# Key parts of a head pair by one copy, one subtraction and six transfers; value low parts in one operation; probability rows 4 to 11 scaled by GpSimd instead of ScalarE

## The chip, the cores and the metric

One NeuronCore of a Trainium2 chip. The metric is the device time of one execution in microseconds (us): the median of 3 runs before the change is 721.15 us (719.63 to 722.5). The engines have short names: PE is TensorE, DVE VectorE, ACT ScalarE, POOL GpSimd, SP SyncE (it only issues transfers here). Each engine has its own stream of instructions and works through it in order; semaphores hold an instruction back until what it reads is there.

## The reference

One transformer block on 512 tokens of width 1024, all in float32. Layer norm, a modulation computed from a condition vector, one input projection; then eight heads of dilated attention (group A) and eight heads of three-branch attention (group B: compressed, selected and window keys); output projection, residual, layer norm; a gated feed-forward layer of width 2816 with a causal convolution; residual and layer norm.

```python
mod = silu(c) @ w_ada + b_ada
u = layer_norm(x) * (1 + sc1) + sh1
qa, ka, va, qb, kc, vc, ksl, vsl, kw, vw, gl = split(u @ w_in)
o_a = dilated_attention(rope(qa), rope(ka), va)
o_b = nsa_attention(rope(qb), rope(kc), vc, rope(ksl), vsl, rope(kw), vw, gl, ...)
x = layer_norm(ALPHA * x + g1 * (concat(o_a, o_b) @ w_o), ln1_g, ln1_b)
u = layer_norm(x) * (1 + sc2) + sh2
a_gate, a_val = split(u @ w_up)
h = gelu(causal_dwconv(a_gate)) * a_val
x = layer_norm(ALPHA * x + g2 * (h @ w_down), ln2_g, ln2_b)
```

## The kernel before, in words

**Split products.** A float32 product is made of three matmuls (`mm3`): each operand is split into a high part (a copy rounded to the narrower type fp32r) and a low part (the operand less its high part), and high times high, high times low and low times high are added up in PSUM. The high part is made by ACT with a copy, the low part by DVE or POOL with a subtraction that reads the high part.

**Stages.** Up to about 52 us the first projection (tile `first`). From there to about 313 us the attention: the rest of the input projection (`quad`, in chunks of 48 matmuls of 256 columns), the rows of attention, and at the end the first output tile. Then output projection, feed-forward (`pg`, `pvv`) and down projection (`d`).

**Rows.** A row is one head, one kind of keys and one or two tiles of 128 queries: 12 rows for each head pair of group B, 6 for each of group A. A row goes through steps: `scores` (PE, lines 707 and 708: queries against `khh` and `kll`), `weights` (DVE, line 715: mask, minimum along the row), `power` (ACT, line 721), `scale` (DVE reciprocal at line 726, then the product with one over the sum and the gate: on ACT at line 732 with one more DVE operation at line 730 where `r['act']` is set, otherwise in one POOL operation at line 736), `turn` (PE transposes, line 741), `parts` and `rest` (ACT and DVE, lines 760 and 764: high and low part of the turned row) and `use` (PE, line 789: products with the values). `SEQ` at line 154 says in which order one round of the loop at line 1303 runs the steps of different rows; `scale` runs one round and `turn` three rounds behind `weights`. Score tiles have two PSUM banks (tag `s`), so the scores of a row start when a bank has been read.

**Key tiles.** A pair of heads shares one PSUM tile `pt`, head 0 on partitions 0 to 63, head 1 on 64 to 127. The scores need for each head a tile `khh` with the head's high part on both halves of the partitions, and a tile `kll` with its low part on both. `k_half` (line 474) makes them for one head: ACT copies 64 partitions (line 478), DVE subtracts on the same 64 (line 480), and one transfer each, issued on SP, brings the half to the other 64 partitions. `k_stack` (line 490) does it for both heads: the two pairs of group B at lines 1284 and 1287; `a_post` (line 945) for the four pairs of group A, one head in each step.

**Value tiles.** `v_split` (line 501) makes, for two heads, high, low, low, high blocks of 64 columns: one ACT copy and two DVE subtractions (lines 505 and 506), twelve times in all (`vb`, `va`).

**Order.** The program is emitted by loops with fillers between the steps (`fill_one`, `run_misc`), and the framework's scheduler sets the final order on every engine. SP's queue carries the weight loads and the key transfers in one stream. The loads of `ada_col` feed reductions on DVE (line 1033), which stand in DVE's stream between the rows' operations.

Of the kernel before, what the change touches and what calls it, by code (L numbers as in the profile page):

```python
# [14 lines left out]
AF = mybir.ActivationFunctionType  # L15
# [91 lines left out]
def body(ctx, tc, nc, a, out, dbg=None):  # L107
# [59 lines left out]
    V, A, P, T = nc.vector, nc.scalar, nc.gpsimd, nc.tensor  # L167
# [58 lines left out]
    def acc_done():  # L226
        live[0] -= 1
# [8 lines left out]
    def f(x):  # L236
        return x.bitcast(F32)

    def load(dst, src, queue=nc.sync):
        queue.dma_start(dst, src)  # L240
# [114 lines left out]
    _, uh, ul = u_parts()  # L355
# [110 lines left out]
    def q_stack(pt, mk=t2):  # L466
# [4 lines left out]
        V.tensor_sub(o[0:64], pt[64:128], f(o[64:128]))  # L471
        return e, o

    def k_half(pt, e, mk=t2, spare=True):
        b, c0 = 64 * e, 64 - 64 * e
        if spare:
            hh, ll = mk('khh'), mk('kll')
            A.activation(hh[b:b + 64], pt[b:b + 64], AF.Copy)
            load(f(hh[c0:c0 + 64]), f(hh[b:b + 64]))
            V.tensor_sub(ll[b:b + 64], pt[b:b + 64], f(hh[b:b + 64]))  # L480
            load(f(ll[c0:c0 + 64]), f(ll[b:b + 64]))
            return hh, ll
        hh, ll = mk('khh'), mk('kll')
        A.activation(hh[b:b + 64], pt[b:b + 64], AF.Copy)
        A.activation(hh[c0:c0 + 64], pt[b:b + 64], AF.Copy)
        V.tensor_sub(ll[b:b + 64], pt[b:b + 64], f(hh[b:b + 64]))
        V.tensor_copy(ll[c0:c0 + 64], f(ll[b:b + 64]))
        return hh, ll

    def k_stack(pt, mk=t2):  # L490
        return [k_half(pt, e, mk) for e in range(2)]


    gates = cst.tile([128, NT, 24], F32, name='gates')
# [6 lines left out]
    def v_split(dst, src, n):  # L501
        s4 = src.rearrange("p (n e d) -> p n e d", e=2, d=64)
        d4 = dst.rearrange("p (n s d) -> p n s d", s=4, d=64)
        A.activation(d4[:, :, 0:4:3, :], s4, AF.Copy)
        V.tensor_sub(d4[:, :, 1, :], s4[:, :, 0, :], f(d4[:, :, 0, :]))
        V.tensor_sub(d4[:, :, 2, :], s4[:, :, 1, :], f(d4[:, :, 3, :]))


    def blocks_of(src, eng, res):
# [435 lines left out]
    def a_post(j):  # L945
        mk = to if j == 0 else t2

        def run(banks):
# [15 lines left out]
            pt = transposed(ys, 1, 'acc')  # L964
            wlive[0] -= 2
            yield 2
            ka[j] = []
            for b in range(2):
                ka[j].append(k_half(pt, b, mk))
                if b == 1:  # L970
                    acc_done()
                    ready.add(('a', j))
                yield
        return run

    def a_head(j, e):
# [317 lines left out]
        start_misc(late_steps(GAP, st_))  # L1294
    nrow = len(rows)
    for k, r in enumerate(rows):
        r['act'] = 4 <= k < 20
    rows[0]['scores']()
    wo_started = [False]
    wo_fill = wo_first()  # L1300
# [261 lines left out]
```

## Time and profile before

| | us |
|---|---|
| median of 3 runs | 721.15 (719.63 to 722.5) |
| the profiled execution | 724.09 |
| its span, first to last instruction | 722.3 |
| PE busy in the span | 692.0 |
| DVE, ACT, POOL busy | 459.2, 347.3, 238.7 |

The profiled execution is one more execution of the same program; its span leaves out 1.8 us around the first and the last instruction. A timeline row gives start, duration, engine, line and operation; a bracket at its end gives how long the engine had been idle before it and what ended that. A row of a table of stretches gives busy time and count of instructions for each engine in a stretch, then the granted share of TensorE's full clock, the busy share of the 16 DMA engines and what they moved.

### The profile page before, as it was taken

What the parts mean: (1) busy time and instruction counts of PE and PEld (TensorE: products, weight loads), DVE (VectorE), ACT (ScalarE), POOL (GpSimd) and SP (SyncE); (2) the same over time, 40 slices, a digit from 0 to 9 for tenths busy, and PEclk for the clock granted to TensorE, in tenths of its full rate; (3) what the DMA queues carried; (4) which work ended last, traced back from release to release, by engine and by line L of the source; (5) the groups of instructions that cost most, each with busy time, mean ns of one, the idle gap of its engine ahead of it and who ended that gap; (6) DMA issues with size and microseconds to landing.
All of it is one profiled execution on the core that took longest, in us unless ns stands there. A gap on an engine that the chain in (4) does not pass through costs nothing.

```text
span 722.3 us, 10901 instructions
## 1 busy us (share of the span) xinstructions
PE 692.0 (96%) x3964; PEld 598.6 (83%) x3964; DVE 459.2 (64%) x965; ACT 347.3 (48%) x706; POOL 238.7 (33%) x252
## 2 busy tenths in 40 slices
PE   8999899899989998999999999999999999999995
PEld 7999689897889886778898888888888788888884
DVE  7879877767886989978844444554543363445236
ACT  5657487744567588916553333333433341232101
POOL 2002510342466484512310110111110355765326
PEclk8999999999999999999999999999999999999999
DMA  9967741256451212350112233444423233434002
GB/s 343 386 207 197 208 144 68 59 204 234 146 204 60 59 61 87 130 192 1 59 59 88 88 100 133 142 147 148 146 91 114 88 110 123 139 123 136 10 15 102
DMA packets 31069, 93.07 MB, mean 129 GB/s; under 512 B 4132, under 2 KB 4900, under 8 KB 31016
## 3 DMA queue, kind: packets, MB, share of 16 engines
q1 hardware_dynamic: 30580, 92.20, 37.8%
q8 instruction: 31, 0.51, 0.3%
q10 hardware_dynamic: 436, 0.18, 0.1%
q14 instruction: 22, 0.18, 0.1%
HBM read 87.13 MB, written 2.10 MB: 124 GB/s over the span
## 4 chain that ended last, share of the span: by engine, by line
PE 75%; DVE 11%; ACT 5%; POOL 3%; issue 3%; DMA 2%; POOLq 0%; SPq 0%; DVEq 0%; ACTq 0%
PE d L261 6%; PE d L260 6%; PE d L259 6%; PE pvv L259 5%; PE pvv L261 5%; PE pvv L260 5%; PE pg L259 5%; PE pg L261 5%; PE pg L260 5%; PE first L393 3%; PE quad L259 3%; PE quad L260 2%; PE quad L261 2%; PE pT L741 2%; PE hid L1160 2%
## 5 line engine op out<-in xcount | busy, mean ns | idle before, releaser
L256 DVE TENSOR_TENSOR wlo<-wraw,whi 128x1024 fp32r<-128x1024 f32 x60 | 83.7, 1395 | 122.6 <-ACT whi L255 121.4
L255 ACT ACTIVATE whi<-wraw 128x1024 fp32r<-128x1024 f32 x60 | 63.6, 1060 | 139.9 <-PE pg L260 68.1
L259 PE MATMUL quad<-whi,u 128*128 128x256 f32 x256 | 75.8, 296 | 1.0 <-DVE qo L471 1.0
L260 PE MATMUL quad<-wlo,u 128*128 128x256 f32 x256 | 73.1, 286 | 0.0
L261 PE MATMUL quad<-whi,u 128*128 128x256 f32 x256 | 73.0, 285 | 0.0
L1514 POOL TENSOR_TENSOR wraw<-wraw,arow 128x1024 f32<-128x1024 f32 x22 | 58.9, 2688 | 37.0 <-DMA wraw<-w_down 35.8
L259 PE MATMUL pg<-u,whi 128*128 128x512 f32 (+1 forms) x176 | 67.7, 385 | 0.0
L260 PE MATMUL pg<-u,whi 128*128 128x512 f32 (+1 forms) x176 | 66.8, 380 | 0.0
L261 PE MATMUL pg<-u,wlo 128*128 128x512 f32 (+1 forms) x176 | 66.8, 379 | 0.0
L261 PE MATMUL pvv<-u,wlo 128*128 128x512 f32 (+1 forms) x176 | 66.8, 379 | 0.0
L259 PE MATMUL pvv<-u,whi 128*128 128x512 f32 (+1 forms) x176 | 66.8, 379 | 0.0
L260 PE MATMUL pvv<-u,whi 128*128 128x512 f32 (+1 forms) x176 | 66.8, 379 | 0.0
L256 POOL TENSOR_TENSOR hl<-cv,hh 128x512 fp32r<-128x512 f32 x14 | 23.8, 1704 | 110.6 <-ACT hh L255 110.6
L259 PEld LDWEIGHTS quad<-whi,u 128*128 128x128 f32 x256 | 49.5, 193 | 5.8 <-issue 3.9
L260 PEld LDWEIGHTS quad<-wlo,u 128*128 128x128 f32 x256 | 49.5, 193 | 1.1 <-issue 0.4
L715 DVE CUSTOM_DVE_ANT_0 p<-sp,masks 128x128 f32<-128x128 f32 (+1 forms) x96 | 44.6, 482 | 8.6 <-PE sp L708 8.2
L261 PEld LDWEIGHTS quad<-whi,u 128*128 128x128 f32 x256 | 49.5, 193 | 0.1
L741 PE MATMUL pT<-ident,p 128*128 128x128 f32 x240 | 39.9, 280 | 7.4 <-POOL p L736 4.1
L260 PEld LDWEIGHTS pg<-u,whi 128*128 128x128 f32 x176 | 33.1, 188 | 6.7 <-issue 0.5
L259 PEld LDWEIGHTS pg<-u,whi 128*128 128x128 f32 x176 | 33.1, 188 | 6.5 <-issue 0.5
L261 PEld LDWEIGHTS pg<-u,wlo 128*128 128x128 f32 x176 | 33.1, 188 | 6.3
L260 PEld LDWEIGHTS pvv<-u,whi 128*128 128x128 f32 x176 | 33.1, 188 | 6.2
(650 smaller groups left out, 1855.3 us busy)
## 6 DMA issues: line engine op xcount, KB each, us to landing
wraw<-w_up SPq DMA_DIRECT2D x44, 512.0 KB, 3.2
wraw<-w_down SPq DMA_DIRECT2D x22, 512.0 KB, 3.3
ada<-ada_col SPq DMA_DIRECT2D x32, 256.0 KB, 5.8
wraw<-w_quad SPq DMA_DIRECT2D x16, 512.0 KB, 4.3
wraw<-ada_col SPq DMA_DIRECT2D x16, 512.0 KB, 4.3
wraw<-ada_row SPq DMA_DIRECT2D x16, 512.0 KB, 3.3
x<-x SPq DMA_DIRECT2D x8, 512.0 KB, 4.9
wraw<-w_o SPq DMA_DIRECT2D x8, 512.0 KB, 3.2
```

The costliest lines, as they stand in the source:

```text
L255: A.activation(hi, raw, AF.Copy)
L256: lo_engine.tensor_sub(lo, raw, f(hi))
L259: T.matmul(o_, sh, mh, start=start, stop=False)
L260: T.matmul(o_, sh, ml, start=False, stop=False)
L261: T.matmul(o_, sl, mh, start=False, stop=stop)
L393: T.matmul(o_, l[:, tk], r[:, cs], start=(j == 0 and t % 2 == 0 and x == 0 and term is terms[0]), stop=(j == KD - 1 and t % 2 == 1 and x = ...
L715: V.tensor_tensor_reduce(p[:, cols[i]], e['s'][:, cols[i]], masks[:, m0:mask0 + 512], 1.0, 3e38, op0=ALU.add, op1=ALU.min, accum_out=m_[:, ...
L741: T.transpose(e['t'][:, 128 * j:128 * j + 128], e['p'][:, 128 * j:128 * j + 128], ident)
L1160: T.matmul(acc[0:62, 0:256], bl[l_ // 8][:, l_ % 8, :], w[:, l, :], start=l_ == 0, stop=l_ == 15)
L1514: P.tensor_mul(w, w, g2)
```

## The change

Three edits. (1) `k_pair` makes the tiles of both heads of a pair together: ACT copies all 128 partitions of `pt` into the second head's high tile, DVE subtracts all 128 into the second head's low tile, and six transfers spread them: for high and low each, the lower half goes to both halves of the first head's tile, and then the upper half of the second head's tile goes over its own lower half. That third transfer overwrites what the first two read, so it waits until both have landed. `a_post` now calls it in one step, frees the PSUM bank there, and says that the pair is ready one step later. (2) `v_split` subtracts both low blocks in one DVE operation. (3) `r['act']` is set for rows 12 to 19 instead of 4 to 19, so rows 4 to 11 are scaled at POOL's line.

```diff
--- before.py
+++ after.py
@@ -471,6 +471,17 @@
         V.tensor_sub(o[0:64], pt[64:128], f(o[64:128]))
         return e, o
 
+    def k_pair(pt, mk=t2):
+
+        a_, b_ = [mk('khh') for _ in range(2)], [mk('kll') for _ in range(2)]
+        A.activation(a_[1], pt, AF.Copy)
+        V.tensor_sub(b_[1], pt, f(a_[1]))
+        for x in (a_, b_):
+            for h in range(2):
+                load(f(x[0][64 * h:64 * h + 64]), f(x[1][0:64]))
+            load(f(x[1][0:64]), f(x[1][64:128]))
+        return list(zip(a_, b_))
+
     def k_half(pt, e, mk=t2, spare=True):
         b, c0 = 64 * e, 64 - 64 * e
         if spare:
@@ -488,7 +499,7 @@
         return hh, ll
 
     def k_stack(pt, mk=t2):
-        return [k_half(pt, e, mk) for e in range(2)]
+        return k_pair(pt, mk)
 
 
     gates = cst.tile([128, NT, 24], F32, name='gates')
@@ -502,8 +513,7 @@
         s4 = src.rearrange("p (n e d) -> p n e d", e=2, d=64)
         d4 = dst.rearrange("p (n s d) -> p n s d", s=4, d=64)
         A.activation(d4[:, :, 0:4:3, :], s4, AF.Copy)
-        V.tensor_sub(d4[:, :, 1, :], s4[:, :, 0, :], f(d4[:, :, 0, :]))
-        V.tensor_sub(d4[:, :, 2, :], s4[:, :, 1, :], f(d4[:, :, 3, :]))
+        V.tensor_sub(d4[:, :, 1:3, :], s4, f(d4[:, :, 0:4:3, :]))
 
 
     def blocks_of(src, eng, res):
@@ -964,13 +974,11 @@
             pt = transposed(ys, 1, 'acc')
             wlive[0] -= 2
             yield 2
-            ka[j] = []
-            for b in range(2):
-                ka[j].append(k_half(pt, b, mk))
-                if b == 1:
-                    acc_done()
-                    ready.add(('a', j))
-                yield
+            ka[j] = k_pair(pt, mk)
+            acc_done()
+            yield
+            ready.add(('a', j))
+            yield
         return run
 
     def a_head(j, e):
@@ -1294,7 +1302,7 @@
         start_misc(late_steps(GAP, st_))
     nrow = len(rows)
     for k, r in enumerate(rows):
-        r['act'] = 4 <= k < 20
+        r['act'] = 12 <= k < 20
     rows[0]['scores']()
     wo_started = [False]
     wo_fill = wo_first()
```

The scheduler's order moves with it. Lines from 482 on have other numbers in the changed program (before/after): 1033/1041, 1125/1133, 715/725, 736/746, 519/529; 480 becomes 478.

SP's queue around the two pairs of group B, before:

```order
L240 DMA wraw<-ada_col 128x1024
L240 DMA khh<-khh 64x512
L240 DMA kll<-kll 64x512
L240 DMA khh<-khh 64x512
L240 DMA kll<-kll 64x512
L240 DMA khh<-khh 64x512
L240 DMA wraw<-w_quad 128x1024
L240 DMA kll<-kll 64x512
L240 DMA khh<-khh 64x512
L240 DMA kll<-kll 64x512
L240 DMA wraw<-ada_col 128x1024 x2
```

and now:

```order
L240 DMA wraw<-ada_col 128x1024
L240 DMA khh<-khh 64x512 x2
L240 DMA kll<-kll 64x512 x2
L240 DMA wraw<-w_quad 128x1024
L240 DMA khh<-khh 64x512
L240 DMA kll<-kll 64x512
L240 DMA khh<-khh 64x512 x2
L240 DMA kll<-kll 64x512 x2
L240 DMA wraw<-ada_col 128x1024
L240 DMA khh<-khh 64x512
L240 DMA kll<-kll 64x512
L240 DMA wraw<-ada_col 128x1024
```

The first two transfers of high and low parts now stand together, and the third ones behind a load of weights (`w_quad`, `ada_col`).

DVE in the same place, before (`kll` is the subtraction for keys, `qe` and `qo` for queries, the operation that writes `wraw,mod` a reduction over `ada_col`, `p,sa__982` the first row's weights):

```order
L1033 ISA wraw,mod<-wraw,crow,b_col 128x1024
L1033 ISA mod 128x1
L480 TENSOR_TENSOR kll<-qT,khh 64x512
L1125 TENSOR_TENSOR wlo<-wraw,whi 128x512
L470 TENSOR_TENSOR qe<-qT,qe 64x512
L471 TENSOR_TENSOR qo<-qT,qo 64x512
L480 TENSOR_TENSOR kll<-qT,khh 64x512
L1033 ISA wraw,mod<-wraw,crow,b_col 128x1024
L1033 ISA mod 128x1
L480 TENSOR_TENSOR kll<-qT,khh 64x512
L470 TENSOR_TENSOR qe<-qT,qe 64x512
L471 TENSOR_TENSOR qo<-qT,qo 64x512
```

and now:

```order
L1041 ISA wraw,mod<-wraw,crow,b_col 128x1024
L1041 ISA mod 128x1
L1133 TENSOR_TENSOR wlo<-wraw,whi 128x512
L1041 ISA wraw,mod<-wraw,crow,b_col 128x1024
L1041 ISA mod 128x1
L470 TENSOR_TENSOR qe<-qT,qe 64x512
L471 TENSOR_TENSOR qo<-qT,qo 64x512
L478 TENSOR_TENSOR kll<-qT,khh 128x512
L1133 TENSOR_TENSOR wlo<-wraw,whi 128x512
L725 ISA p,sa__982<-sp,masks 128x128
L725 ISA sa__982 128x1
L725 ISA p,sa__982<-sp,masks 128x256
```

Of three key subtractions in this piece one is left (a fourth stands just ahead of it in both orders, as 64 and now as 128 partitions). The second reduction stands before the queries' subtractions instead of behind them, a subtraction of weights (`wlo`) has come in behind the keys, and the second pair of `qe` and `qo` has gone behind the weights of the first two rows.

POOL around 200 us (`p` of the first rows of the third head pair; `wlo` is the low part of a weight chunk), before:

```order
L736 TENSOR_SCALAR p<-p,sa__2447 128x128
L736 TENSOR_SCALAR p<-p,sa__2447 128x256
L736 TENSOR_SCALAR p<-p,sa__2478 128x384
L1125 TENSOR_TENSOR wlo<-wraw,whi 128x512 x2
L736 TENSOR_SCALAR p<-p,sa__2520 128x512
L736 TENSOR_SCALAR p<-p,sa__2557 128x128
```

and now:

```order
L746 TENSOR_SCALAR p<-p,sa__2431 128x128
L746 TENSOR_SCALAR p<-p,sa__2431 128x256
L746 TENSOR_SCALAR p<-p,sa__2462 128x384
L746 TENSOR_SCALAR p<-p,sa__2504 128x512
L1133 TENSOR_TENSOR wlo<-wraw,whi 128x512 x2
L746 TENSOR_SCALAR p<-p,sa__2541 128x128
```

The row of 512 columns now stands ahead of the two subtractions for the weights instead of behind them. Further up, the eight additions for the compressed values (`bst<-vct`), which stood behind row 3 of the attention, now stand behind row 11.

## Rows read from the trace of the kernel before

**Rows 1.** The page: busy time of each engine over the span, and the shares by engine of the chain that ended last.

```profile
PE 692.0 (96%) x3964; PEld 598.6 (83%) x3964; DVE 459.2 (64%) x965; ACT 347.3 (48%) x706; POOL 238.7 (33%) x252
...
PE 75%; DVE 11%; ACT 5%; POOL 3%; issue 3%; DMA 2%; POOLq 0%; SPq 0%; DVEq 0%; ACTq 0%
```

**Rows 2.** Busy time in stretches of 50 us (columns: stretch, its length, busy time and count of PE, weight loads, DVE, ACT, POOL; granted clock, DMA share, GB/s).

```profile
50.00:100.00 50.00, 46.33 (x350) 42.29 (x349) 41.83 (x129) 33.34 (x80) 18.94 (x22) 1.00 0.64 189
...
200.00:250.00 50.00, 46.40 (x371) 45.42 (x371) 39.37 (x115) 31.82 (x83) 30.38 (x40) 0.97 0.30 103
...
250.00:300.00 50.00, 45.90 (x316) 39.50 (x314) 45.93 (x146) 43.48 (x119) 30.34 (x45) 1.00 0.23 69
...
400.00:450.00 50.00, 50.00 (x222) 41.42 (x221) 21.94 (x24) 18.43 (x23) 6.77 (x5) 1.00 0.33 112
```

**Rows 3.** PE's timeline: the first score matmul of attention, and instructions before which PE had been idle.

```profile
69.53 0.22 PE L707 MATMUL sp<-khh,qe 128*128 128x128 f32 x1
...
71.84 0.44 PE L707 MATMUL sp<-khh,qe 128*128 128x384 f32 x1 [0.37 <-DVE qo L471]
...
74.77 0.33 PE L708 MATMUL sp<-kll,qe 128*128 128x128 f32 x1 [0.87 <-DMA kll<-kll]
...
81.37 0.50 PE L707 MATMUL sp<-khh,qe 128*128 128x512 f32 x1 [1.29 <-DVE sa__1095 L715]
...
90.50 0.55 PE L741 MATMUL pT<-ident,p 128*128 128x128 f32 x3 [1.08 <-ACT p L732]
...
142.82 0.30 PE L708 MATMUL sp<-kll,qe 128*128 128x128 f32 x1 [0.46 <-DMA kll<-kll]
...
203.33 0.89 PE L741 MATMUL pT<-ident,p 128*128 128x128 f32 x4 [2.32 <-POOL p L736]
...
272.79 0.55 PE L741 MATMUL pT<-ident,p 128*128 128x128 f32 x3 [1.38 <-DVE pTl L764]
```

**Rows 4.** DVE's timeline around the first rows of attention.

```profile
65.61 0.69 DVE L1125 TENSOR_TENSOR wlo<-wraw,whi 128x512 fp32r<-128x512 f32 x1
...
68.36 1.27 DVE L1033 CUSTOM_DVE_ANT_0 wraw<-wraw,crow,b_col 128x1024 f32<-128x1024 f32 x1
...
69.67 0.69 DVE L480 TENSOR_TENSOR kll<-qT,khh 64x512 fp32r<-64x512 f32 x1
...
70.39 0.69 DVE L470 TENSOR_TENSOR qe<-qT,qe 64x512 fp32r<-64x512 f32 x1
...
71.82 0.29 DVE L715 CUSTOM_DVE_ANT_0 p<-sp,masks 128x128 f32<-128x128 f32 x1
...
77.67 1.29 DVE L1033 CUSTOM_DVE_ANT_0 wraw<-wraw,crow,b_col 128x1024 f32<-128x1024 f32 x1 [2.87 <-DMA wraw<-ada_col]
...
80.90 0.41 DVE L715 CUSTOM_DVE_ANT_0 p<-sp,masks 128x256 f32<-128x256 f32 x1
```

**Rows 5.** Loads and key transfers: SP's timeline; the chain that ended last, from the issue of an `ada_col` load to its landing (start, us); the instructions on tile `khh` (min/median/max in ns) and the time from issue to landing of its transfers; and the stretch in which the DMA engines are busiest, with the columns of rows 2.

```profile
61.85 0.33 SPq L240 DMA_DIRECT2D wraw<-ada_col  x1
...
70.90 6.63 DMA wraw<-ada_col
...
L478 ACT ACTIVATE khh<-qT x12: 575/592/595, 61.8 to 278.7; 64x512 fp32r<-64x512 f32 x12
...
L240 SPq DMA_DIRECT2D khh<-khh x12: 462/468/547, 62.4 to 279.3; - x12
...
L480 DVE TENSOR_TENSOR kll<-qT,khh x12: 672/688/695, 62.8 to 279.3; 64x512 fp32r<-64x512 f32 x12
...
DMA to landing us min/median/max: 2.2/2.3/6.9
...
64.00:76.00 12.00, 10.76 (x85) 10.10 (x84) 10.52 (x27) 9.26 (x22) 8.53 (x11) 1.00 1.00 216
```

**Rows 6.** POOL's timeline at 196 to 203 us, DVE's reduction in the same stretch, and POOL's timeline at 219 us.

```profile
195.99 2.14 POOL L736 TENSOR_SCALAR p<-p,sa__2478 128x384 f32<-128x384 f32 x1 [0.36 <-DVE sa__2478 L726]
...
198.13 3.51 POOL L1125 TENSOR_TENSOR wlo<-wraw,whi 128x512 fp32r<-128x512 f32 x2
...
201.61 1.66 POOL L736 TENSOR_SCALAR p<-p,sa__2520 128x512 f32<-128x512 f32 x1
...
201.45 1.27 DVE L1033 CUSTOM_DVE_ANT_0 wraw<-wraw,crow,b_col 128x1024 f32<-128x1024 f32 x1
...
219.24 0.66 POOL L736 TENSOR_SCALAR p<-p,sa__2829,gates 128x384 f32<-128x384 f32 x1
...
219.88 0.77 POOL L736 TENSOR_SCALAR p<-p,sa__2869,gates 128x512 f32<-128x512 f32 x1
```

**Rows 7.** The stretch behind PE's longest idle time, with the columns of rows 2.

```profile
203.60:207.00 3.40, 3.40 (x18) 3.40 (x17) 3.09 (x10) 0.60 (x1) 1.04 (x3) 0.50 0.89 333
```

**Rows 8.** Instructions of single lines (min/median/max in ns): the scaling on ACT for rows of 128 and 256, 384 and 512 columns, the gate's product on DVE, and the first of the two value subtractions.

```profile
L732 ACT ACTIVATE p<-p,sa__1204 x2: 385/438/492, 94.7 to 95.0; 128x128 f32<-128x128 f32 x1, 128x256 f32<-128x256 f32 x1
...
L732 ACT ACTIVATE p<-p,sa__1128 x1: 616/616/616, 89.8 to 89.8; 128x384 f32<-128x384 f32 x1
...
L732 ACT ACTIVATE p<-p,sa__1164 x1: 726/726/726, 91.8 to 91.8; 128x512 f32<-128x512 f32 x1
...
L730 DVE TENSOR_TENSOR sa__1128<-sa__1128,gates x1: 681/681/681, 89.1 to 89.1; 128x1 f32<-128x1 f32 x1
...
L505 DVE TENSOR_TENSOR vb<-quad,vb x4: 271/284/292, 72.4 to 80.5; 128x128 fp32r<-128x128 f32 x4
```

## The prediction

> **What bounds the kernel now.** I read the page first. The reader is to see two things in it: PE is busy for 692.0 of 722.3 us, and the chain that ended last is PE's own work for 75% and DVE's for 11% [rows 1]. So nothing that shortens DVE, ACT or POOL counts by itself; it counts where PE stands idle and the chain leaves PE. The stretches of 50 us say where that is: from 400 to 450 us PE never stops, while from 50 to 100, 200 to 250 and 250 to 300 us it stands still for 3.67, 3.60 and 4.10 us [rows 2]. The change works in these stretches alone. The most that it can win is the idle time there, plus time at a lower clock. PE's timeline then gives each larger wait its place and the engine that ended it [rows 3]: 0.37, 0.87, 1.29 and 1.08 us among the first rows of attention, 0.46 us at the first scores of group A, 2.32 us at 203 us for a row that POOL scales, 1.38 us at 272 us for DVE. The timelines of DVE, SP and POOL were read last, for what stands ahead of the operation that ended the wait. At 250 to 300 us DVE is busy for 45.93 and ACT for 43.48 of 50 us [rows 2]; there they set the pace themselves.
>
> **The change part by part.** I work against the profiled execution's own 724.09 us (span 722.3 and 1.79 around it), which lies 2.94 above the median of the runs; a difference is then taken from the median.
>
> *Counts.* A key copy on ACT takes 592 ns and a key subtraction on DVE 688 ns for 64 partitions and 512 columns [rows 5]. I take the same for 128 partitions: a full-height copy or subtraction of 512 columns in this trace has the same kind of duration (a weight's low part, 128x512, took 0.69 us [rows 4]). Six pairs lose six of each: 3.6 us of ACT, 4.1 us of DVE. The value subtractions took 284 ns for 128 columns [rows 8]; twelve pairs of them become twelve operations of 256 columns, which I put at 0.41 us as the weights of 256 columns [rows 4], so 0.16 us each and 1.9 us of DVE in all. Rows 4 to 11 are three rows of 384 columns, three of 512 and two of 128 and 256. ACT loses 3 x 0.616 + 3 x 0.726 + 4 x 0.438 = 5.8 us, and DVE eight products, of which the first took 0.68 us [rows 8]. POOL gains 3 x 0.66 + 3 x 0.77 + 2 x 1.0 = 6.3 us, by rows of these sizes where nothing disturbs them [rows 6]; the 1.0 is for 128 and 256 columns in two operations, put between one and two of the 0.66. SP gets twelve more issues of 0.47 us [rows 5]. All of this is hidden where PE is fed; only the places below count.
>
> *First rows of attention, 64 to 92 us.* Here the DMA engines are busy for all of the 12 us from 64 to 76, and a key transfer, 2.3 us in the median, takes up to 6.9 [rows 5]. DVE's order moves too. Its fourth reduction over `ada_col`, asked for at 61.85 [rows 5], stood behind the queries' subtractions and ran at 68.36 without a wait [rows 4]; it now stands ahead of them. DVE is there at about 65.6, one key subtraction (0.69) earlier than it ended `wlo` before. The data land at 64.1 at the earliest (shortest landing, 2.2) and 68.4 at the latest. So DVE stands there for nothing to 2.8 us; I take the late end, since the transfers of this stretch are slow. Then come the reduction (1.3), `qe`, `qo`, one key subtraction and one `wlo` (0.69 each): the first row's weights start at 72.4 at the latest, 0.6 later than 71.82 [rows 4]. PE's first scores need `qe`, so they start at about 70.4 instead of 69.53 [rows 3], and the second row's wait about 0.7 us for the bank that the first row's weights free. That is 1.6 us of new waiting in place of the 0.37.
>
> What goes: the 0.87 us wait for `kll` was for the second pair's low part, which came last of four subtractions; now it comes from the second of two, and three more matmuls stand ahead of its reader. The 1.29 us came from DVE, which stood 2.87 us at a reduction waiting for the `ada_col` load issued at 70.90 [rows 4, 5], with the third row's weights behind it. That load is now issued behind both low parts, near 72.9, and DVE reaches its reduction some 3 us later, near 78, so what is left of the wait is 0 to 1.4 us. From the first row's weights to the end of row 3's it was 81.31 - 71.82 = 9.5 us; now it is 9.5 + 0.69 (`wlo`) + 1.38 (`qe`, `qo`) - 1.3 (a reduction that is now earlier) - 0.6 (four value tiles) - 2.87 + 0.7 = 7.5. So DVE is done at 79.9 instead of 81.31, and PE, with 1.6 instead of 2.53 us of waiting, is there at 80.4 and need not wait. Then the 1.08 us: row 4's scaling stood behind a gate product of 0.68 us on DVE and a copy on ACT [rows 3, 8]; now POOL does both in 0.66 [rows 6], and DVE's earlier work comes 1.4 us sooner. Gain 0.9 + 1.1 = 2.0; I take 1.5, since four more transfers go through a stretch with full DMA engines. Bounds: all four waits gone, 3.6 won; or the transfers late, 2.9 lost (worked out below).
>
> *First pair of group A, 142 us.* The pair's parts come 0.5 to 1 us later, by two more issues on SP [rows 5]. But four matmuls of the compressed keys and twelve of a projection now stand ahead of the scores that waited 0.46 us [rows 3], and they cover that. Gain 0.46, bounds 0 and 0.46. Second heads get their tiles one landing later, 2.3 to 6.9 us; they are read three rows later.
>
> *POOL at 196 to 203 us.* The row of 512 columns waited for two low parts of weights, 3.51 us; that is PE's 2.32 us [rows 3, 6]. In the new order it stands ahead of them. The next row then waits for them, but its transposes stand on PE behind its own scores and some twenty matmuls of the projection, so I expect only 0.5 us of waiting there. Gain 1.8; bounds 0 and 2.32. Behind this wait TensorE ran at a granted clock of 0.50, the lower level of 1.2 GHz, for 3.4 us [rows 7]; if it stays at the upper level, 1.7 us more are won. I leave that out of the sum and keep it in the range.
>
> *245 to 300 us.* Two pairs are made here. DVE, the busiest beside PE, loses 2 x 0.69. Some of PE's waits are for it (the 1.38 us [rows 3]), some for POOL and ACT; I take half, 0.7, with bounds 0 and 2.6 (DVE's and ACT's share both).
>
> Sum: 1.5 + 0.46 + 1.8 + 0.7 = 4.5 us. The profiled execution would become 719.6, and the median 721.15 - 4.5 = 716.7 us.
>
> **The rivals.** *Transfers late (slower).* The third transfer of a part holds SP's queue until the first two have landed; behind it stand the second pair's transfers and the `ada_col` load that DVE waits for. If that takes the 6.9 us of the slowest transfer here [rows 5], then the first pair's are issued at 62.4 and 0.47 later, land at 69.8, the second pair's go out behind them near 70.8 and land at 77.7: 2.9 us behind 74.77, when PE had the second pair before [rows 3]. A wait of 2.9 us is longer than the one which was followed by 3.4 us at half the clock [rows 3, 7], so 1.7 is added. I count no gain elsewhere with it, since the waits behind it move along with PE: 721.15 + 4.6 = 725.8. It decides from a landing of about 5 us on. For it speaks the full DMA share; against it that SP's new order has half as many loads between the keys, and that most landings of key transfers took 2.3.
>
> *POOL held by DVE.* A POOL row of 384 columns took 2.14 instead of 0.66 us, and one of 512 columns 1.66 instead of 0.77, each while DVE ran a reduction over two operands in SBUF [rows 6]. Rows 4 to 6 would be scaled on POOL while DVE runs such reductions. If two of them meet one, 1.5 + 0.9 us, the 1.08 us stays and another 1.3 comes: the sum falls to 2.1 and the time is 719.0. Against it: the scaling has two rounds before its transposes. The Trainium skill says of this, on the page "SBUF — State Buffer", section "Who interferes with whom", that a DVE instruction with two SBUF inputs and a GpSimd instruction that reads SBUF exclude each other for a whole instruction. The trace agrees, with 2.14 against 0.66 us, and that rule speaks against the move to POOL.
>
> *The waits come again.* Most of PE's order has moved; a stretch at which an engine is as full as DVE here may give new waits for those that go. If all but a tenth comes back, 720.7.
>
> *All of it, and the clock:* 3.6 + 0.46 + 2.3 + 1.7 = 8.1, that is 713.
>
> **How the numbers follow.** Forecast 0.47, transfers late 0.16, POOL held 0.16, waits again 0.13, all of it 0.08. A measurement of this kernel tells about 0.5% from no change, 3.6 us: below 717.5 is faster, above 724.8 slower. The forecast's own range is 714 to 719; three quarters of its chance lie below 717.5. Faster: 0.35 + 0.08 = 0.43. Same: 0.12 + 0.16 + 0.13 = 0.41. Slower: 0.16. The range runs from 712.0, the best case with a little room, to 724.5, which leaves out most of the slower case.
>
> **What would show it.** Right: no wait of PE over 0.6 us for POOL's scaling near 200 us and none of half the clock behind it; DVE's wait at the reduction moved from near 75 us to near 66; the wait for `kll` near 74 us and the one for row 4's scaling near 90 us gone. Wrong: a wait of PE for `khh` or `kll` of over 1 us among the first six rows (transfers late); POOL's scaling of rows 4 to 11 above 1.2 us with PE's transposes behind it (POOL held); the idle time from 50 to 300 us as long as before, in other places (waits again). The forecast falls if PE's idle time there shrinks by less than 2 us.

## The result, and the profile after

The changed kernel took 716.47 us in the median of 4 runs (716.19 to 717.68), against 721.14 us (719.63 to 722.5) for the kernel before beside it: a ratio of 0.9938, with a 95% interval of 0.9916 to 0.9961. The forecast was 716.7. In a second sitting the same kernel stood at 0.9947 [0.9929, 0.9966]. So it is faster, by 0.6 and 0.5%, with intervals that reach from 0.3 to 0.8%. The profiled execution took 716.19 us with a span of 714.4.

The page of after, its busy times and its chain that ended last, which answer to [rows 1]:

```profile
PE 688.3 (96%) x3964; PEld 596.2 (83%) x3964; DVE 449.6 (63%) x939; ACT 339.6 (48%) x690; POOL 243.2 (34%) x262
...
PE 76%; DVE 12%; ACT 4%; issue 3%; POOL 2%; DMA 2%; POOLq 0%; SPq 0%; DVEq 0%; ACTq 0%
```

DVE is busy for 9.6 us less and ACT for 7.7, POOL for 4.5 more, and the median is 4.7 us lower. These numbers should not yet be connected: the experiments show a kernel that is as fast without the saved operations.

The stretches of 50 us, with the columns of [rows 2]:

```profile
50.00:100.00 50.00, 48.16 (x365) 44.21 (x365) 39.91 (x119) 31.16 (x76) 18.12 (x23) 1.00 0.63 201
200.00:250.00 50.00, 47.61 (x390) 46.52 (x391) 39.75 (x127) 33.77 (x94) 31.12 (x43) 1.00 0.32 101
250.00:300.00 50.00, 45.22 (x300) 37.96 (x298) 47.01 (x126) 44.26 (x111) 29.16 (x41) 1.00 0.35 111
400.00:450.00 50.00, 50.00 (x223) 41.38 (x222) 22.31 (x25) 18.86 (x24) 8.08 (x5) 1.00 0.34 116
```

PE is busy for 1.8 us more in the first stretch and 1.2 more in the second, and for 0.7 less in the third; from 400 us on nothing has changed. (The same microsecond holds somewhat later work in after, since it runs ahead of before by up to 7.6 us.)

PE's timeline of after, the larger waits, which answer to [rows 3]:

```profile
71.30 0.33 PE L717 MATMUL sp<-khh,qe 128*128 128x128 f32 x1 [1.45 <-DVE qo L471]
...
135.20 0.63 PE L462 MATMUL qT<-ident,yq 128*128 128x128 f32 x4 [1.24 <-DVE qo L471]
...
162.04 0.36 PE L259 MATMUL quad<-whi,u 128*128 128x256 f32 x1 [0.92 <-DVE qo L471]
...
177.62 0.41 PE L630 MATMUL vcp<-cin,gd 128*128 128x64 f32 x2 [1.30 <-DVE gd L623]
...
201.32 0.44 PE L751 MATMUL pT<-ident,p 128*128 128x128 f32 x2 [1.09 <-POOL p L746]
...
265.94 0.55 PE L751 MATMUL pT<-ident,p 128*128 128x128 f32 x3 [1.66 <-DVE pTl L774]
```

Gone are the waits for `kll` at 74 and 142 us, for DVE at 81 and for row 4's scaling at 90 us; new are the 1.45 us at the first scores and the 0.92 at 162; one wait of 1.30 at 177 us for the gate's products `gd` stands in place of three at 180 to 185 us (0.95, 0.28 and 1.47), of which this is the last, from PE's timeline of before:

```profile
185.44 0.44 PE L462 MATMUL qT<-ident,yq 128*128 128x128 f32 x2 [1.47 <-POOL yq L427]
```

The 2.32 us at 203 became 1.09, and it now belongs to the next row (`sa__2541`, 128 and 256 columns).

DVE's timeline of after at the first rows, which answers to [rows 4]:

```profile
65.07 0.69 DVE L1133 TENSOR_TENSOR wlo<-wraw,whi 128x512 fp32r<-128x512 f32 x1
...
68.25 1.55 DVE L1041 CUSTOM_DVE_ANT_0 wraw<-wraw,crow,b_col 128x1024 f32<-128x1024 f32 x1 [2.50 <-DMA wraw<-ada_col]
...
70.55 0.69 DVE L471 TENSOR_TENSOR qo<-qT,qo 64x512 fp32r<-64x512 f32 x1
...
72.48 0.28 DVE L725 CUSTOM_DVE_ANT_0 p<-sp,masks 128x128 f32<-128x128 f32 x1
...
78.62 1.28 DVE L1041 CUSTOM_DVE_ANT_0 wraw<-wraw,crow,b_col 128x1024 f32<-128x1024 f32 x1 [0.73 <-DMA wraw<-ada_col]
```

DVE's wait has moved from 77.67 [rows 4] to 66, and PE's first scores pay for it.

### The profile page after: what moved, and what is told of

The parts are those of the page before. It is cut to its first block, busy times and chain, and to the rows that moved or that the text cites. A ratio compares the mean times of both kernels' runs of the same rounds, so it can differ in the third digit from the quotient of the medians.

```text
span 714.4 us, 10895 instructions
## 1 busy us (share of the span) xinstructions
PE 688.3 (96%) x3964; PEld 596.2 (83%) x3964; DVE 449.6 (63%) x939; ACT 339.6 (48%) x690; POOL 243.2 (34%) x262
## 4 chain that ended last, share of the span: by engine, by line
PE 76%; DVE 12%; ACT 4%; issue 3%; POOL 2%; DMA 2%; POOLq 0%; SPq 0%; DVEq 0%; ACTq 0%
PE d L260 6%; PE d L259 6%; PE d L261 6%; PE pvv L261 5%; PE pvv L260 5%; PE pvv L259 5%; PE pg L261 5%; PE pg L260 5%; PE pg L259 5%; PE quad L259 3%; PE first L393 3%; PE quad L260 3%; PE quad L261 3%; PE pT L751 2%; PE pvb L799 2%
## 5 line engine op out<-in xcount | busy, mean ns | idle before, releaser
L256 DVE TENSOR_TENSOR wlo<-wraw,whi 128x1024 fp32r<-128x1024 f32 x60 | 79.4, 1323 | 126.4 <-ACT whi L255 125.5
L1522 POOL TENSOR_TENSOR wraw<-wraw,arow 128x1024 f32<-128x1024 f32 x22 | 61.0, 2786 | 33.9 <-DMA wraw<-w_down 29.3
L256 POOL TENSOR_TENSOR hl<-cv,hh 128x512 fp32r<-128x512 f32 x14 | 21.7, 1551 | 111.1 <-ACT hh L255 111.1
```

The source lines that it names most:

```text
L256: lo_engine.tensor_sub(lo, raw, f(hi))
L1522: P.tensor_mul(w, w, g2)
```

## Two tables from PE's timelines

Twelve more kernels were run, one of them the whole change again; "values only", "ready late" and so on are explained with the experiments. To compare their profiled executions I add up PE's idle times of over 0.1 us by place (us from the start of the span), in us. The last column is time at a granted clock of about 0.50, the lower level of 1.2 GHz, between 60 and 600 us: the start and length of each such stretch. It costs at most half its length, and that much if PE is busy all through it.

| kernel | first rows 60-95 | 130-148 | 154-191 | 191-212 | 236-258 | 258-316 | clock 0.50 |
|---|---|---|---|---|---|---|---|
| before | 3.61 | 1.92 | 2.70 | 2.32 | 1.53 | 5.51 | 187: 3.4, 204: 3.4 |
| values only | 1.27 | 1.79 | 2.90 | 2.31 | 1.52 | 5.53 | none |
| rows only | 1.82 | 1.69 | 2.94 | 2.31 | 1.54 | 5.56 | none |
| pairs of B only | 3.37 | 1.49 | 3.03 | 2.32 | 1.54 | 5.58 | 201: 3.4 |
| keys only | 2.27 | 1.25 | 3.05 | 1.09 | 1.30 | 4.60 | 180: 3.4, 269: 3.4 |
| order only | 1.88 | 1.23 | 2.45 | 0.80 | 1.52 | 5.52 | 180: 3.4 |
| order and rows | 2.73 | 1.24 | 2.07 | 0.73 | 1.52 | 5.56 | 179: 3.4 |
| keys and rows | 1.64 | 1.26 | 2.97 | 1.09 | 1.30 | 5.27 | 180: 3.4 |
| whole (first) | 1.84 | 1.24 | 2.22 | 1.09 | 1.30 | 5.40 | 179: 3.4 |
| whole (again) | 3.09 | 1.25 | 3.30 | 1.31 | 1.30 | 5.23 | 179: 6.8 |
| before, low parts on DVE | 2.91 | 1.73 | 2.55 | 1.61 | 1.53 | 5.52 | 276: 3.4 |
| ready late | 1.69 | 1.23 | 4.26 | 0.90 | 1.52 | 5.52 | 178: 10.2 |
| one step | 0.87 | 1.52 | 5.07 | 2.01 | 1.53 | 5.54 | 185: 6.8 |
| whole, low parts on DVE | 2.63 | 1.25 | 4.05 | 0.18 | 1.30 | 5.26 | 179: 6.8 |

The second table has the timed runs of some of the kernels in three sittings, each with its own runs of before: mean span, and the time that the clock cost, an estimate worked out as span times (1 - mean granted clock). In the profiled executions, but for that of ready late, the larger part of the time at 0.50 lies in the program's first 21 us and last 8. "Keys only" and "order only" belong to the first sitting, the two with rows and the whole to the second, the last three kernels to the third.

| kernel | span | cost of the clock | rest |
|---|---|---|---|
| before (three sittings) | 719.8, 720.0, 720.1 | 7.0, 7.3, 7.9 | 712.8, 712.7, 712.2 |
| keys only | 717.0 | 7.0 | 710.0 |
| order only | 717.4 | 7.1 | 710.3 |
| order and rows | 716.2 | 6.0 | 710.2 |
| keys and rows | 716.2 | 6.4 | 709.8 |
| whole | 716.6 | 7.6 | 709.0 |
| whole, low parts on DVE | 715.8 | 6.5 | 709.3 |
| ready late | 722.0 | 9.9 | 712.1 |
| one step | 723.6 | 8.2 | 715.3 |

## The experiments

*One edit at a time.* The key edit alone (`k_pair`, and the step in which a pair of group A is made), the value edit alone and the rows edit alone:

```diff
+            ka[j] = k_pair(pt, mk)          keys only
+            acc_done()
+            yield
+            ready.add(('a', j))
+            yield
...
+        V.tensor_sub(d4[:, :, 1:3, :], s4, f(d4[:, :, 0:4:3, :]))          values only
...
+        r['act'] = 12 <= k < 20          rows only
```

> Only the key edit of the change (one copy, one subtraction, six transfers, and the step of a_post). Theory A, the prediction's sum: this edit carries the places at 64 to 82, at 142, at 203 and at 245 to 300 us, since it is the one that moves the orders of DVE, SP and POOL there; the wait at 90 us for row 4's scaling stays. 3.2 to 4.0 us less than before, ratio about 0.995. Rival B, relief of the busy engines: each edit wins in proportion to the DVE time that it frees, 4.1 of 8.3 us, so about half of the change's 4.7 us: 2.3 us, ratio 0.997. Rival C, transfers late: with the transfers the edit alone is no gain, ratio 1.000 or above, and the gain comes from rows 4 to 11.

> Only the value edit (one subtraction of 256 columns instead of two of 128). PE's order is nearly that of before. Theory A: no place of the sum depends on it, ratio 1.000 within 0.001. Rival B: 1.9 of 8.3 us of DVE freed, so about 1.1 us less, ratio 0.9985.

> Only the row edit (rows 4 to 11 scaled on POOL). PE's order is that of before, word for word. Theory A: the wait of 1.08 us at 90 us goes, the others stay: 1.1 us less, ratio 0.9985. Rival B: 2.3 of 8.3 us of DVE freed and 5.8 us of ACT, 1.3 us or more less. Rival D, POOL held by DVE's reductions: 0 to 2 us more than before, with scaling of over 1.2 us on POOL at 80 to 92 us.

Measured: keys 0.9964 [0.9947, 0.9981], values 1.0002 [0.9984, 1.0021], rows 0.9991 [0.9974, 1.0009]. The value edit gives nothing that can be measured, though twelve times two subtractions of 0.28 us become twelve of 0.42, 1.7 us less of DVE. The rows edit gives nothing that can be measured by itself; its order on PE is that of before, and its trace shows the wait for row 4's scaling at 90 us gone. About six tenths of the gain are the key edit's (0.36 of 0.5 to 0.6%); the interval does not tell theory A from rival B. But that edit does two things: it saves copies and subtractions, and it moves steps. `a_post` is a generator, and each `yield` ends one of its steps. Before, the first step makes one head's parts, and the second makes the other's, gives the PSUM bank back and tells that the pair is ready. Now the first step makes both heads' parts and gives the bank back, and the second tells that the pair is ready. So the pair is told ready one step behind its parts, but in the same step as before; what comes one step earlier is the second head's parts and the bank.

*The order alone.* Both `k_half` of a pair of group A in the first step, the bank given back there, the pair told ready in the second step, as before. No copy, subtraction or transfer is saved:

```diff
-            ka[j] = []
-            for b in range(2):
-                ka[j].append(k_half(pt, b, mk))
-                if b == 1:
-                    acc_done()
-                    ready.add(('a', j))
-                yield
+            ka[j] = [k_half(pt, b, mk) for b in range(2)]
+            acc_done()
+            yield
+            ready.add(('a', j))
+            yield
```

> None of the three edits: before with its own copies, subtractions and four transfers, but a_post makes both heads in one step, frees the bank there and reports one step later, as the change does. POOL's order at 200 us becomes that of the changed kernel (the 512-column row ahead of the two weight subtractions). Theory A: the 2.3 us wait at 203 us shrinks to about 0.5 as with the whole change, and the first rows of attention stay as before: 1.8 us less, up to 3.5 if the half clock behind that wait goes too. Rival E, a reshuffled order by itself is worth what the change is worth: about 4.7 us less, or a change of any sign with no wait gone at 203 us.

> The whole change once more, in the same sitting as the next three, so that they can be set side by side. Measured so far 0.9938 with an interval from 0.9916 to 0.9961. If the edits add up (keys alone 0.9964, rows alone 0.9991, values alone 1.0002) it comes at 0.9957; if the edits help each other it stays near 0.994.

Measured, the order alone: 0.9967 [0.9948, 0.9986], the same as keys only, which has the saved operations too. (The whole once more, in the second sitting: 0.9947 [0.9929, 0.9966]. The 0.9957 of the three edits added up lies within, so it is not shown that they help each other.) PE's and POOL's timelines of the order alone:

```profile
178.43 0.41 PE L620 MATMUL vcp<-cin,gd 128*128 128x64 f32 x2 [1.54 <-DVE gd L613]
...
199.84 0.68 PE L789 MATMUL pva<-pT,va 128*128 128x256 f32 x4 [0.55 <-DVE fold L856]
```

```profile
194.23 1.94 POOL L736 TENSOR_SCALAR p<-p,sa__2520 128x512 f32<-128x512 f32 x1 [2.42 <-ACT p L721]
196.14 3.51 POOL L1123 TENSOR_TENSOR wlo<-wraw,whi 128x512 fp32r<-128x512 f32 x2
```

The row of 512 columns stands ahead of the two low parts here too, PE's wait of 2.32 us is gone, and so is the 0.46 at 142 us. These two places are the order's, not those of the saved operations.

*The pairs of group B.* `k_pair` there alone, where the step stays as it was, so that saved operations and the moved reduction are all that is tried:

```diff
-        return [k_half(pt, e, mk) for e in range(2)]
+        return k_pair(pt, mk)
```

> The key edit for the two pairs of group B alone; the four pairs of group A are made as before, one head in each step. DVE's order at 64 to 72 us is that of the changed kernel, POOL's order at 200 us that of before. Theory A as the prediction had it: the first rows of attention win 0.9 us and nothing else, ratio 0.9988. Theory F, after the first four runs: what counts is a_post's step and POOL's order, and at the first rows the new waits for the queries' subtractions eat up what goes: 1.000 within 0.001, with one wait of about 1.4 us near 70 us and the 2.3 us wait at 200 us still there.

Measured: 0.9984 [0.9969, 0.9999], 0.2% at the edge of what can be told, and by the total nearer to theory A (0.9988) than to theory F (1.000). But PE's idle time at the first rows was 3.37 us, with 2.23 at the first scores: the part of the change at which the forecast saw 1.5 us gives no shorter waits there. Some 0.3 us of the total are at the end of the program (below).

*Sums without one part.* The order with the rows edit, and the whole without the value edit:

> The order-only kernel with rows 4 to 11 on POOL: no operation of the key edit and none of the value edit. Theory F: 0.996, the two single effects added (0.9967 and 0.9991), within 1.5 us of the whole change. Theory A: it lacks the freed DVE and ACT time at 245 to 300 us and the first rows' gain, so it stays 1.6 us behind the whole change.

> The whole change without the value edit. Values alone were worth nothing, so both theories expect the whole change's time within 0.7 us, ratio 0.994 to 0.996. POOL's order at 200 us has the 512-column row ahead of the weight subtractions only there and no longer at the next chunk; if the wait at 200 us is the one that matters, that makes no difference.

Measured: 0.9946 [0.9924, 0.9967] and 0.9943 [0.9920, 0.9965], beside 0.9947 for the whole in that sitting. Order and rows, with no operation of a key or a value saved, come out level with the whole. Each interval is 0.2% to either side, so a difference of up to some 2 us, theory A's 1.6 among them, could not be told. (Rows add 0.002 to the order, which is less than the intervals can tell.)

*Is it POOL at 200 us?* Before, with the low parts of that one projection made by DVE:

```diff
-                    (V if i < 6 else P).tensor_sub(
+                    (V if i < 7 else P).tensor_sub(
```

> The kernel before, with one edit: the low parts of the weights of one projection, the one whose two low parts ran on POOL at 198 us (and a third at 215), are made by DVE. Theory that PE's 2.32 us wait at 203 us is POOL's two low parts standing ahead of the row of 512 columns: the wait there falls below 0.6 us, the idle time of PE from 192 to 210 us from 2.3 to about 0.6, ratio 0.997 to 0.998. Rival, that the wait only has another owner (DVE, which gets three subtractions of 0.69 us): over 1.5 us of idle time stays from 192 to 210, with DVE as its releaser, ratio 0.999 to 1.002.

Measured: 0.9991 [0.9971, 1.0012]. PE's timeline of it:

```profile
202.23 0.44 PE L741 MATMUL pT<-ident,p 128*128 128x128 f32 x2 [0.56 <-POOL p L736]
...
208.05 0.66 PE L741 MATMUL pT<-ident,p 128*128 128x128 f32 x4 [0.78 <-POOL p L736]
```

The cause of that wait is shown: without the two low parts the 2.32 us are 0.56. But 0.78 us for POOL comes behind it, and the idle time of that place is 1.61, not the 0.6 expected: the rival's amount, though the owner is still POOL and not DVE. The theory of the wait was right, its price was not: this cure alone is worth 0.7 us of idle time, less than can be measured.

*When is the pair told ready?* First, the pair told ready one step later than before, its heads still made in two steps; then both heads in one step and the pair told ready there, one step earlier than before. Both were meant as the two halves of the order, but they are not: the order tells the pair ready in the second step, like before, the one of these kernels in the third and the other in the first.

```diff
-                    ready.add(('a', j))
                 yield
+            ready.add(('a', j))
+            yield
```

```diff
+            ka[j] = [k_half(pt, b, mk) for b in range(2)]
+            acc_done()
+            ready.add(('a', j))
+            yield
```

> The kernel before, with one edit: a pair of group A still makes its two heads' parts in two steps, but is told ready one step later. No operation is saved. Theory that the whole gain of the order comes from the later ready (POOL's two low parts fall behind the row of 512 columns): idle time 133 to 146 us about 1.25, 192 to 210 us about 0.8, ratio 0.996 to 0.998. Rival, that it comes from making both heads in one step: ratio 0.999 to 1.001.

> The kernel before, with the other half of that edit: both heads' parts of a pair of group A in one step, told ready at once. No operation is saved. One of POOL's low parts stands between the rows of 384 and of 512 columns, the other ahead of the row of 384. Theory of the later ready: the idle time from 192 to 210 us stays above 1.5, ratio 0.999 to 1.001. Rival, that one step is what counts: idle time there below 1.2, ratio 0.996 to 0.998.

Measured: 1.0017 [0.9990, 1.0044] and 1.0052 [1.0032, 1.0072]. Neither theory holds for the total: neither kernel gains, and the one that tells earlier is slower by 0.5%. What was not run is the order's own half: both heads in the first step with the bank given back in the second, which would part the earlier parts from the earlier bank. For the places the later ready does what was expected: 1.23 us from 130 to 148, 0.90 from 191 to 212. What they gain is lost between. PE's and POOL's timelines of the kernel with the later ready, its stretches behind that wait (columns of [rows 2]), and DVE's timeline:

```profile
179.06 0.69 PE L462 MATMUL qT<-ident,yq 128*128 128x128 f32 x2 [2.87 <-POOL yq L427]
```

```profile
175.54 1.48 POOL L424 TENSOR_TENSOR rt<-yq,rope 128x128 f32<-128x128 f32 x1 [2.67 <-ACT yq L450]
...
177.70 1.31 POOL L427 TENSOR_TENSOR yq<-rt 128x128 f32<-128x128 f32 x1
```

```profile
178.10:181.40 3.30, 2.33 (x12) 2.34 (x13) 3.30 (x9) 0.91 (x3) 0.91 (x1) 0.50 0.84 233
181.50:184.80 3.30, 3.08 (x16) 2.92 (x16) 3.08 (x8) 2.56 (x5) 0.00 (x0) 0.50 0.90 205
184.90:188.20 3.30, 3.30 (x16) 3.23 (x16) 2.96 (x9) 1.23 (x5) 0.00 (x0) 0.50 0.97 289
```

```profile
175.43 1.28 DVE L1034 CUSTOM_DVE_ANT_0 wraw<-wraw,crow,b_col 128x1024 f32<-128x1024 f32 x1 [6.54 <-issue]
...
177.35 1.35 DVE L1034 CUSTOM_DVE_ANT_0 wraw<-wraw,crow,b_col 128x1024 f32<-128x1024 f32 x1
```

PE stood for POOL's rotation of a projection, of which two operations took 1.48 and 1.31 us while DVE ran the two `ada_col` reductions shown last (the same two took 0.46 each at 171 us, with no reduction beside them). From 178.1 us on, while PE still stood, the clock was at 0.50 for 10.2 us; PE was busy for 9.0 of them, so some 4.5 us were lost. The timed runs show less of it: without the clock's cost this kernel stands at 712.1, like before; the clock costs it 2.0 us more than before in the same sitting. So it gained at two places, lost at a third, and lost by the clock. With one step, PE's timeline at the same place and at 203 us:

```profile
186.56 0.69 PE L462 MATMUL qT<-ident,yq 128*128 128x128 f32 x2 [3.00 <-POOL yq L427]
...
203.86 0.55 PE L741 MATMUL pT<-ident,p 128*128 128x128 f32 x3 [2.01 <-DVE pT L764]
```

Here the wait for the rotation is 3.00 us, and the wait at 203 us has only another owner.

*Whole, and the low parts on DVE.*

> The changed kernel, and in addition the low parts of that one projection made by DVE. If the 1.09 us that PE still waits near 200 us is POOL's two low parts, it falls below 0.5, and the ratio is 0.002 below that of the changed kernel, 0.992 to 0.994. Rival: DVE is as full as PE there and the time comes back elsewhere between 192 and 310 us, ratio 0.994 to 0.996.

Measured: 0.9942 [0.9917, 0.9967], the same as the whole. The 1.09 us at 200 us fell to 0.18, as expected, and nothing came of it that can be measured; the two theories' ratios meet at 0.994 and are not told apart. DVE's and PE's timelines of this kernel, and then of the whole in its second profile:

```profile
178.17 1.28 DVE L1041 CUSTOM_DVE_ANT_0 wraw<-wraw,crow,b_col 128x1024 f32<-128x1024 f32 x1 [1.97 <-DMA wraw<-ada_col]
...
179.75 0.66 PE L630 MATMUL vcp<-cin,gd 128*128 128x64 f32 x2 [3.21 <-DVE gd L623]
```

```profile
177.63 1.28 DVE L1041 CUSTOM_DVE_ANT_0 wraw<-wraw,crow,b_col 128x1024 f32<-128x1024 f32 x1 [0.90 <-DMA wraw<-ada_col]
...
179.45 0.66 PE L630 MATMUL vcp<-cin,gd 128*128 128x64 f32 x2 [2.38 <-DVE gd L623]
```

These are the products `gd` standing behind a reduction whose load is late. It is one place, and PE waited 1.30 and 2.38 us there in two executions of the whole and 3.21 in this kernel; the stretch at half the clock beside it was 3.4 us long in the first and 6.8 in the other two. A second profile of the same kernel thus moves by more (1.1 us of waiting and 3.4 of half clock) than what the fix at 200 us took away (0.9).

## Why the prediction was right, and where it was not

The time and its range were right. That PE's idle places are where the change works was right in the main; the sum of their prices came out by some luck, for a term that is not shown made up for gains that the forecast did not have. By the steps:

*Counts.* Right. A key copy of full height took 592 ns and its subtraction 688, a value subtraction of 256 columns 420, as taken. A pair of value subtractions became shorter by 0.14 us, not 0.16, so 1.7 us of DVE went and not 1.9. Of the eight rows moved to POOL seven took 0.66, 0.77 or 0.98 us, by their size, as taken; one was slowed, row 5 by 0.81, as was row 3, which POOL had before, by 0.95:

```profile
81.98 1.93 POOL L746 TENSOR_SCALAR p<-p,sa__1091,gates 128x128 f32<-128x128 f32 x2 [0.34 <-DVE sa__1091 L736]
...
88.01 1.58 POOL L746 TENSOR_SCALAR p<-p,sa__1160,gates 128x512 f32<-128x512 f32 x1 [2.96 <-DVE sa__1160 L736]
```

That is the rival "POOL held by DVE" in its mechanism, but PE did not wait for either row, so it cost nothing at the place named. The mechanism weighed at another place, POOL's rotation: at 176 us in ready late, and at 183 us in one step, where two operations of it took 1.13 and 1.70 us beside reductions.

*First rows, the mechanism.* Right nearly to the tenth. DVE was at the moved reduction at 65.75 us (65.6 forecast), its data came at 68.25 (68.4), the first row's weights started at 72.48 (72.4); PE waited 1.45 us (1.6) for the queries; DVE's second wait shrank from 2.87 to 0.73 (0 to 1.4). All of the old waits went in this execution.

*First rows, the gain of 1.5 us.* This is the step that failed, by size: the 1.5 us are not shown. It took PE's 3.61 us of one profiled execution as what before costs. Six more kernels with the reduction where it stands in before had 1.27, 1.82, 1.88, 1.69, 0.87 and 2.73 us, and the one with the low parts on DVE 2.91; with before that is 2.1 in the mean. Six executions with DVE's new order there had 1.64 to 3.37, 2.5 in the mean. So the change has no shown gain at the first rows. Together the waits that went were longer in that one execution of before than in any other with this order, and the wait for the moved reduction (1.43 to 2.24 us at the first scores) takes their place.

*142 us.* Right: the 0.46 us are gone in all seven executions of kernels with the order of the whole (keys, order, whole).

*POOL at 200 us.* Right in place and direction: 0.5 us of waiting was expected for the next row, 1.09 came, so 1.23 was gained and not 1.8. The sign that the forecast set itself here, no wait over 0.6 us for POOL's scaling, was thus not met. What it left out is that the moved row ran no faster itself: POOL's row took 2.04 us and the next 1.80 (0.77 and 0.98 undisturbed), each while DVE ran an `ada_col` reduction. Before it was the same [rows 6]; DVE's timeline of before has the reduction that ran beside the row of 2.14 us:

```profile
196.40 1.27 DVE L1033 CUSTOM_DVE_ANT_0 wraw<-wraw,crow,b_col 128x1024 f32<-128x1024 f32 x1
```

POOL's and DVE's timelines of after:

```profile
193.85 2.04 POOL L746 TENSOR_SCALAR p<-p,sa__2504 128x512 f32<-128x512 f32 x1 [1.22 <-DVE sa__2504 L736]
195.86 3.63 POOL L1133 TENSOR_TENSOR wlo<-wraw,whi 128x512 fp32r<-128x512 f32 x2
199.47 1.80 POOL L746 TENSOR_SCALAR p<-p,sa__2541 128x128 f32<-128x128 f32 x2
```

```profile
194.07 1.26 DVE L1041 CUSTOM_DVE_ANT_0 wraw<-wraw,crow,b_col 128x1024 f32<-128x1024 f32 x1
...
199.60 1.32 DVE L1041 CUSTOM_DVE_ANT_0 wraw<-wraw,crow,b_col 128x1024 f32<-128x1024 f32 x1
```

The half clock of [rows 7] did not come behind this wait in any of the seven executions of kernels with the order of the whole; it came at the wait at 177 us in its place, in all of them. The timed runs show no sure gain from the clock: it costs the whole 7.6 us and before 7.3 in the same sitting.

*245 to 300 us.* 0.7 us were expected of DVE's saved subtractions, 0.3 to 0.5 came in the whole (236 to 258: 1.53 to 1.30; 258 to 316: 5.51 to 5.40 and 5.23), 1.1 in keys only, and only kernels with `k_pair` for group A show it. For the whole, half the cut of a busy engine was too much: the waits there are ended in turn by DVE and POOL.

*What the forecast did not have.* First, PE's own time, from the first projection to the first transposes of the output (`quad` at 54 to 56 us to `x1T` at 317 to 325), without idle times and without half of what PE was busy at the lower clock. For the same 1784 matmuls it is 246.6 to 247.1 us in the five executions with `k_pair` for group A (the whole twice, keys only, keys and rows, the whole with low parts on DVE). In the nine others it is 247.3 to 249.3: 248.2 in before, 248.0 in values only, 248.4 in rows only, 247.3 in the order alone and in ready late, 248.3 in order and rows, 249.3 in before with low parts on DVE. Order and rows is as fast as the whole with 248.3, and the profile models the ends of matmuls, so this term is not settled to better than 1 us. Second, 0.3 us at the very end: from the issue of the last store to the end of the span it is 2.54 us in all six executions with `k_pair`, 2.85 to 2.88 in the eight others. There SP waits for the semaphores of the transfers one after the other, about 0.06 us each. Without `k_pair` the last store's semaphore is the first of five in that row, and four more waits follow its landing; with the added transfers it is the fifth, and the others are done by then. That is most of the 0.3 us.

*The sum.* In place of 1.5 + 0.46 + 1.8 + 0.7 stand about 0 + 0.5 + 1.2 + 0.4 of idle time, 1.4 of PE's own time and 0.3 at the end. That is 3.8 us, between the 4.7 of the first sitting and the 3.5 of the second. One term was too large by about as much as was missing, which is luck. The forecast was to fall if PE's idle time from 50 to 300 us shrank by less than 2 us. In the two profiles it went from 15.9 to 12.5. But values only, rows only and before with low parts on DVE have 13.8 to 14.3 there, and the whole in its second profile has 14.1: by the means, 14.6 against 13.3, it shrank by 1.3.

*The rivals.* Transfers late came true in its condition and not in its price. SP's timeline of after, and the time from issue to landing of the transfers on tile `khh`:

```profile
68.97 0.46 SPq L240 DMA_DIRECT2D khh<-khh  x1
...
70.48 1.20 SPq L240 DMA_DIRECT2D khh<-khh  x2
...
DMA to landing us min/median/max: 2.2/2.4/5.7
```

The first pair's transfers took up to 5.7 us, the third was held until 68.97, and the second pair's went out at 70.48, where the rival put them near 70.8. But these landed after 2.6 to 3.8 us and not after 6.9, and PE's wait at the first rows was for `qo` and none over 0.1 us for `khh` or `kll`. The reduction's load behind them went out at 74.42 instead of 72.9, at a price of the 0.73 us that DVE waited. Waits come again did in part, at 162 and 177 us, where kernels with the new order have 2.1 to 4.1 us idle and those with the order of before 2.6 to 3.0.

Open is why the second head's parts and the bank, one step earlier, gain what they gain, and why telling the pair ready a step later or earlier than before does not. The rows tell where (PE's place behind POOL's rotation or the gate's products at 176 to 187 us), not a rule by which it could have been said ahead. For the slower one the profile shows 5.07 us of idle time there against 2.6 to 3.0, while its timed runs are 3 us longer without the clock's cost.

## What to carry to other kernels

An edit that saves work on engines off the path and also moves the step in which work is issued is two edits. Run the order without the saving before crediting the saving: here it had all of what the key edit gave, as far as the intervals tell, and with the rows edit as much as the whole change. When an edit of the order is taken apart, write down for each part in which step every action falls, before and after; here two runs meant as halves were none. Take the idle time of a place from several executions, or from kernels which share its order, before it becomes a term: one profile of before showed 3.6 us where the mean was 2.1. When one wait is cured, look at the next row of the same engine; here it kept a third to a half of it.

## What was not expected of the hardware

Stretches at a granted clock of 0.50 come or stay away between executions of kernels that wait alike: behind the same 2.3 us at 200 us one came in before and in the pairs of B, none in values only and rows only. At 176 to 179 us they lasted for 3.4 us at waits of 1.30 to 2.59 us (five executions), for 6.8 at 2.38 and 3.21, and for 10.2 at 2.87: no length of the wait tells them apart. A stretch of 3.4 us costs up to 1.7 us. They are only a part of the spread between executions: the 35 runs of before in the first sitting spread by 1.5 us (standard deviation of the span), and still by 1.4 without the clock's cost. The same matmuls take PE between 246.6 and 249.3 us in the orders tried here, with idle time and clock taken out; how much of that lies in the ends that the profile models is not shown.
